# Split weight parts that start at seven places within a 64-byte line

## The chip, the core and the metric

The kernel runs on one core of a Trainium2 chip. The metric is the device time of one execution in microseconds. The core has a matrix engine (TensorE, PE in the profile, with its weight loads listed as PEld), a vector engine (VectorE, DVE), a scalar engine (ScalarE, ACT), a general engine (GpSimd, POOL) and a queue that issues transfers (SyncE, SP). Operands lie in an on-chip memory of 128 partitions (SBUF), results of matmuls in another (PSUM).

## The reference, cut to what matters

Two layers of a decoder trunk over 512 tokens of width 1024, in float32. Each layer is a chain of weight products with attention, a retention branch and gates between them:

```
for l in range(DEPTH):                       # DEPTH = 2
    h  = rmsnorm(x, g_mix)
    z  = h @ w_in                            # 1024 -> 5888 columns, split in nine
    ya = sliding_window_sink_attention(aq, ak, av, sinks) @ w_a
    yb = (rmsnorm_per_head(retention(rq, rk, rv)) * silu(rg)) @ w_b
    x  = x + (sigmoid(ga) * ya + sigmoid(gb) * yb) @ w_out
    h2 = rmsnorm(x, g_mlp)
    x  = x + square(relu(h2 @ w_up)) @ w_down   # 1024 -> 4096 -> 1024
out = rmsnorm(x, g_final)
```

## The kernel before

**Products in two parts.** A float32 product is made from operands cut in two: hi, the value rounded to the matrix engine's single-pass format (float32r), and lo, what is left of it. `products` (L278 to L286) issues three matmuls for each pair of operands: hi times hi (L284), hi times lo (L285) and lo times hi (L286). Each has a stationary operand of 128 by 128, which is loaded first (an LDWEIGHTS in the profile), and a moving operand of up to 512 columns.

**Weight units.** All weights are laid out beforehand in units of 128 partitions by 1,024 floats (`UNIT`), 4,096 bytes in each partition. `order` lists them in the order of use, 158 for each layer, 316 in all. `load_until` (L171) brings a unit's raw values into a tile with the tag `raw`; `split_until` (L216) makes hi from it on ScalarE (L234) and lo on VectorE (L235); `unit` (L240) hands the two parts to the matmuls and keeps the splits up to three units ahead of use. The tags `raw`, `hi` and `lo` belong to the pool `wpool` (L121), which has three buffers of each. A buffer is written again when the matmuls of the unit that held it are done.

**Where they lie.** In the memory layout of the program before, every buffer of `raw`, `hi` and `lo` starts on a multiple of 64 bytes within its partition, and so do the activations' tiles `x`, `xh`, `xl`, the nine tiles `r0` to `r8`, and the temporaries. Allocation is in steps of 32 bytes; a few constants (`sink`, `mask`, `ident`, `half`) start 32 bytes into a 64-byte line. The constant `LINE` (L50) fills the gains in front of `x` up to a multiple of 16 floats. A slice of 128 columns of a unit begins at a multiple of 512 bytes from the unit's start.

**Who uses the parts.** In most products the weight parts are the stationary operand: `chunk` (L318), `group` (L330), `two_chunks` (L346) and the loop over `w_a` (L897) run them against 512 moving columns of activations. `values` (L742) is the reverse: the activations are stationary and the weight parts move, 512 columns at a time, into four banks named `rv`. In the MLP, `pair` (L1027) works out two blocks of `w_up` by a scheme with seven half products in place of eight; its matmuls have 256 moving columns, and a pair's four parts are units whose raw values are sums and differences that `add_part` (L202) makes on VectorE. There are 14 pairs in each layer. In the last layer's end (`end`, L407) the moving columns are also 256; the last five units of the order get their parts in tiles of their own there, `homes` (L224 to L226), and not in `wpool`.

**Order around the change.** Each engine runs its instructions in program order; waits come from the tiles: ScalarE's L234 waits for a unit's transfer and for a free `hi` buffer, VectorE's L235 for L234, the matmuls for both. Retention and attention steps are put between the products by `advance` (L302). Which instruction comes when doesn't depend on where in a buffer a part starts.

Of the kernel before, what the change touches and what calls it, by code (L numbers as in the profile page):

```python
# [11 lines left out]
F32R = mybir.dt.float32r  # L12
# [5 lines left out]
P = 128  # L18
# [26 lines left out]
UNIT = 1024  # L45
WARM = 8
PACE = 0.8
DEEP = 3
DELAY = 2
LINE = -(-(2 * DEPTH + 1) * KD // 16) * 16  # L50


# [63 lines left out]
def decoder(ctx, tc, xT, x_first, w_in, w_a, w_b, w_out, w_up, w_down, sinks, tables, decay, band, out):  # L116
# [4 lines left out]
    wpool = ctx.enter_context(tc.tile_pool(name="wpool", bufs=3))  # L121
# [6 lines left out]
    def f32(ap):  # L128
        return ap.bitcast(F32)
# [12 lines left out]

    n_gain = LINE
    gain_x = const.tile([P, n_gain + KD * T], F32, name="x")
# [12 lines left out]
    def halves(i):  # L157

        return (slice(0, UNIT // 2), slice(UNIT // 2, UNIT)) if i < 3 else (slice(0, UNIT),)
# [11 lines left out]
    def load_until(n):  # L171
        while state["loaded"] < min(n, len(order)):
            i = state["loaded"]
            layer, name, j = order[i][:3]
            if name == "pair":
                load_part(i)
            else:
                raws[i] = raw_tile()
                for at in halves(i):
                    queue = nc.scalar if i == 0 and at.start == 0 else nc.sync  # L180
                    queue.dma_start(raws[i][:, at], weights[name][layer, j][:, at])
                    if i < 3:
                        load_x()
            state["loaded"] += 1
# [17 lines left out]
    def add_part(i):  # L202
        part = order[i][3]
        if part == 0:
            w2 = raws[i + 3]
            nc.vector.tensor_tensor(raws[i][:, RIGHT], w2[:, RIGHT], w2[:, LEFT], ALU.add)
        elif part == 1:
            w1 = raws[i - 1]
            nc.vector.tensor_tensor(raws[i][:, LEFT], w1[:, RIGHT], w1[:, LEFT], ALU.subtract)
        elif part == 2:  # L210
            raws[i] = big("raw3").rearrange("p a t -> p (a t)")
            w1, w2, z2 = raws[i - 2], raws[i + 1], raws[i - 1]
            nc.vector.tensor_tensor(raws[i][:, LEFT], w1[:, LEFT], w2[:, RIGHT], ALU.subtract)
            nc.vector.tensor_tensor(raws[i][:, RIGHT], z2[:, RIGHT], z2[:, LEFT], ALU.subtract)

    def split_until(n):  # L216
        while state["split"] < min(n, len(order)):
            i = state["split"]
            load_until(i + 3)
            paired = order[i][1] == "pair"  # L220
            if paired:
                add_part(i)
            raw = raws[i]
            if homes and i >= len(order) - len(homes):  # L224
                home = homes[len(order) - 1 - i]
                hi, lo = (home[:, 2 * a : 2 * a + 2, :].rearrange("p a t -> p (a t)") for a in range(2))  # L226
            else:
                hi = wpool.tile([P, UNIT], F32R, tag="hi", name="hi")
                lo = wpool.tile([P, UNIT], F32R, tag="lo", name="lo")
            for at in (LEFT,) if paired and order[i][3] == 3 else halves(i):  # L230
                if i == 0 and at.start == 0:
                    nc.vector.tensor_copy(hi[:, at], raw[:, at])
                else:
                    nc.scalar.activation(hi[:, at], raw[:, at], AF.Copy)  # L234
                nc.vector.tensor_tensor(lo[:, at], raw[:, at], f32(hi[:, at]), ALU.subtract)  # L235
            raws.pop(i - 3 if paired else i, None)
            parts[i] = (hi, lo)
            state["split"] += 1

    def unit(name, layer):  # L240
        i = state["next"]
        assert order[i][:2] == (layer, name), (order[i], layer, name)
        state["next"] += 1
        split_until(i + 3)
        return parts.pop(i)
# [238 lines left out]
    def layer_body(layer):  # L484
# [124 lines left out]
        def attention():  # L609
# [18 lines left out]
            def weighted(n):  # L628
                at = slice(n * P, (n + 1) * P)
                both = big("whole")  # L630
                rest, whole = both[:, 0, :], both[:, 1, :]
                for g in range(N_KV):
                    own, other = slice(64 * g, 64 * g + 64), slice(64 - 64 * g, 128 - 64 * g)
                    po = bank(ps_aux, "pv")
                    kbs = (1,) if n == 0 else (0, 1)
                    for kb in kbs:
                        b = n - 1 + kb
                        cols = slice(b * P, (b + 1) * P)
                        p = 2 * g + kb
                        nc.tensor.matmul(po, v_both[g][:, cols], p_h[:, p, :], start=kb == kbs[0], stop=False)  # L640
                        nc.tensor.matmul(po, v_high[g][:, cols], p_l[:, p, :], start=False, stop=kb == 1)  # L641
                    nc.scalar.activation(rest[own, :], po[other, :], AF.Copy)
                    nc.vector.tensor_tensor(whole[own, :], po[own, :], rest[own, :], ALU.add)
                split(a_h[:, :, at], a_l[:, :, at], whole.rearrange("p (c q) -> p c q", q=P))

            for n in range(NB):
# [3 lines left out]
                for c in range(4):  # L650
# [32 lines left out]
                    pend.append((n, c, sm))  # L683
                    if ready and c == 1 + DELAY:
                        weighted(ready.pop())
# [416 lines left out]

    scaled_input(0, 0)
    split_until(1)
    for u in (2, 3):
        for k in (2 * u - 3, 2 * u - 2):
            scaled_input(k, 0)
        split_until(u)
# [83 lines left out]
def _stack(w, of):  # L1192
    return np.ascontiguousarray(np.stack([np.stack(of(m)) for m in w]))
# [24 lines left out]
def _laid_out(x, g_mix, w_in, sinks, w_a, w_b, w_out, g_mlp, w_up, w_down, g_final):  # L1218
# [8 lines left out]
        "xT": xT,  # L1227
        "x_first": np.concatenate([gains, np.zeros((P, LINE - gains.shape[1]), np.float32), xT[:, 0, :]], 1),
        "w_in": _stack(w_in, _w_in_units),
# [28 lines left out]
```

## Time and profile before

| | |
|---|---|
| median of 3 runs | 1516.12 us (1516.02 to 1518.61) |
| the profiled execution, its own time | 1514.21 us |
| its span, first to last instruction | 1512.4 us |
| mean granted TensorE clock | 0.998 |
| weight loads and matmuls | 8,080 each |
| whole units split on VectorE (L235), mean | 280, 1,222 ns |
| whole units rounded on ScalarE (L234), mean | 280, 1,058 ns |
| half units split on VectorE (L235), mean | 34, 689 ns |
| transfers, mean rate | 155.11 MB, 103 GB/s |

A row of the groups gives the line and engine, the operation, what it writes and reads, the shape, the count, the group's busy time in microseconds and the mean of one in nanoseconds, and then the idle time of the engine just before these instructions with what ended it. Matmuls are pipelined: the duration of one covers its way through the array, and several are under way at once, so that their durations add up to more than the span. How fast they follow each other is read from the start times in the timeline, whose columns are the start and the duration in microseconds, the engine, the line, the operation, what it writes and reads, and the shape.

A table by stretch, of the MLP of the first layer, has for each engine the busy time and the number of instructions:

```profile
core 0: us, PE busy (x) PEld busy (x) DVE busy (x) ACT busy (x) POOL busy (x), PEclk, DMA share, GB/s
520.00:755.00 235.00, 235.00 (x1402) 208.57 (x1401) 154.49 (x208) 104.53 (x147) 0.96 (x1) 1.00 0.32 114
```

### The profile page before, as it was taken

The page shows a single profiled execution, that of the slowest core. Times are in us where ns is not written, and L with a number is a line of the kernel's source. Part 1 is how long each engine was busy: PE and PEld are TensorE (multiplying, and loading weights), DVE is VectorE, ACT ScalarE, POOL GpSimd, SP SyncE. Part 2 cuts the span into 40 slices and gives each one's busy share as a digit, 9 for nine tenths or more (in the row PEclk, how much of TensorE's full clock was granted, in tenths as well). Part 3 has the DMA queues.
Part 4 walks back from the last instruction along what each step waited for, and adds up shares of the span by engine and source line. Part 5 has one row for each costly group of instructions (what it writes and reads, how often), then busy time and mean ns, then how long its engine had stood idle before and what let it go on. Part 6 is the DMA issues. An engine that isn't in the chain of part 4 may idle for free.

```text
span 1512.4 us, 20505 instructions
## 1 busy us (share of the span) xinstructions
PE 1500.7 (99%) x8080; PEld 1293.3 (86%) x8080; DVE 1028.3 (68%) x1598; ACT 738.8 (49%) x1163; POOL 2.9 (0%) x13
## 2 busy tenths in 40 slices
PE   9999999999999999999999999999999999999997
PEld 7888888888888999988888888888888899899997
DVE  7877568754697666676678855677448866766674
ACT  6657355632564444444455742555226544444452
POOL 0000000000000000000000000000000000000000
PEclk9999999999999999999999999999999999999999
DMA  6422222133223232223432222222332222223231
GB/s 220 133 84 70 98 84 91 70 125 126 98 71 111 98 112 98 98 98 127 158 127 91 84 84 95 79 85 84 126 125 91 91 96 97 101 100 110 98 112 57
DMA packets 52784, 155.11 MB, mean 103 GB/s; under 512 B 6352, under 2 KB 8528, under 8 KB 52688
## 3 DMA queue, kind: packets, MB, share of 16 engines
q1 hardware_dynamic: 52544, 153.54, 29.3%
q8 instruction: 63, 1.03, 0.3%
q14 instruction: 33, 0.27, 0.1%
q10 hardware_dynamic: 144, 0.26, 0.0%
HBM read 146.96 MB, written 4.19 MB: 100 GB/s over the span
## 4 chain that ended last, share of the span: by engine, by line
PE 98%; ACT 1%; DVE 0%; DMA 0%; issue 0%; DVEq 0%
PE mm L286 29%; PE mm L284 29%; PE mm L285 29%; PE rv L284 2%; PE rv L286 2%; PE rv L285 2%; PE score L655 1%; PE pT L620 1%; PE r L285 1%; PE r L286 1%; PE r L284 1%; PE pv L641 0%; PE pv L640 0%; PE ssq L378 0%; PE ret L285 0%; PE ret L286 0%
## 5 line engine op out<-in xcount | busy, mean ns | idle before, releaser
L234 ACT ACTIVATE hi<-raw 128x1024 fp32r<-128x1024 f32 (+1 forms) x313 | 314.6, 1013 | 512.2 <-PE mm L285 418.7
L235 DVE TENSOR_TENSOR lo<-raw,hi 128x1024 fp32r<-128x1024 f32 (+1 forms) x314 | 362.9, 1164 | 159.7 <-ACT hi L234 158.9
L285 PE MATMUL mm<-r,hi 128*128 128x512 f32 (+1 forms) x1136 | 391.7, 346 | 0.0
L284 PE MATMUL mm<-r,hi 128*128 128x512 f32 (+1 forms) x1136 | 388.5, 345 | 1.3 <-ACT mm L1041 1.3
L286 PE MATMUL mm<-r,lo 128*128 128x512 f32 (+1 forms) x1136 | 388.4, 346 | 0.0
L284 PE MATMUL mm<-xh,hi 128*128 128x512 f32 (+1 forms) x1008 | 356.9, 356 | 0.5 <-ACT xh L294 0.5
L285 PE MATMUL mm<-xl,hi 128*128 128x512 f32 (+1 forms) x1008 | 356.2, 355 | 0.0
L286 PE MATMUL mm<-xh,lo 128*128 128x512 f32 (+1 forms) x1008 | 355.7, 356 | 0.0
L284 PEld LDWEIGHTS mm<-r,hi 128*128 128x128 f32 x1136 | 212.9, 188 | 29.2 <-ACT mm L1041 1.7
L285 PEld LDWEIGHTS mm<-r,hi 128*128 128x128 f32 x1136 | 213.3, 188 | 28.0
L286 PEld LDWEIGHTS mm<-r,lo 128*128 128x128 f32 x1136 | 213.0, 188 | 26.5
L284 PEld LDWEIGHTS mm<-xh,hi 128*128 128x128 f32 x1008 | 189.4, 188 | 27.3 <-ACT xh L294 1.2
L285 PEld LDWEIGHTS mm<-xl,hi 128*128 128x128 f32 x1008 | 189.4, 188 | 26.9
L286 PEld LDWEIGHTS mm<-xh,lo 128*128 128x128 f32 x1008 | 189.3, 188 | 25.6
L1068 DVE TENSOR_TENSOR x<-x,mm 128x512 f32<-128x512 f32 x56 | 37.9, 687 | 35.0 <-PE mm L286 34.9
L286 PE MATMUL rv<-hi,xl 128*128 128x512 f32 x128 | 50.6, 395 | 0.0
L285 PE MATMUL rv<-lo,xh 128*128 128x512 f32 x128 | 50.5, 395 | 0.0
L284 PE MATMUL rv<-hi,xh 128*128 128x512 f32 x128 | 50.5, 396 | 0.0
L284 PE MATMUL mm<-uhi,hi 128*128 128x512 f32 (+1 forms) x128 | 46.6, 366 | 0.0
L285 PE MATMUL mm<-ulo,hi 128*128 128x512 f32 (+1 forms) x128 | 46.4, 364 | 0.0
L286 PE MATMUL mm<-uhi,lo 128*128 128x512 f32 (+1 forms) x128 | 45.8, 365 | 0.0
L1048 DVE SCALAR_TENSOR_TENSOR z<-mm,rstd 128x256 f32<-128x256 f32 x28 | 11.9, 425 | 39.7 <-PE mm L286 39.7
(188 smaller groups left out, 1683.2 us busy)
## 6 DMA issues: line engine op xcount, KB each, us to landing
raw<-w_in_in SPq DMA_DIRECT2D x89, 512.0 KB, 3.2
raw<-w_down_in SPq DMA_DIRECT2D x64, 512.0 KB, 3.2
raw<-w_up_in SPq DMA_DIRECT2D x36, 512.0 KB, 3.2
raw<-w_up_in SPq DMA_DIRECT2D x56, 256.0 KB, 2.7
raw<-w_b_in SPq DMA_DIRECT2D x16, 512.0 KB, 3.2
raw<-w_out_in SPq DMA_DIRECT2D x16, 512.0 KB, 3.4
raw<-w_a_in SPq DMA_DIRECT2D x8, 512.0 KB, 3.3
x<-xT_in SPq DMA_DIRECT2D x15, 256.0 KB, 3.9
```

The costliest lines, as they stand in the source:

```text
L234: nc.scalar.activation(hi[:, at], raw[:, at], AF.Copy)
L235: nc.vector.tensor_tensor(lo[:, at], raw[:, at], f32(hi[:, at]), ALU.subtract)
L284: nc.tensor.matmul(ps, ah, bh, start=start and i == 0, stop=False, **more)
L285: nc.tensor.matmul(ps, ah, bl, start=False, stop=False, **more)
L286: nc.tensor.matmul(ps, al, bh, start=False, stop=stop and i == n - 1, **more)
L620: nc.tensor.transpose(pt[:, i * P : (i + 1) * P], sm[:, at : at + P], ident)
L655: nc.tensor.matmul(ps[:, g * w : (g + 1) * w], q_s[g][:, c, at], part[:, keys], start=i == 0, stop=i == 1)
L1048: nc.vector.scalar_tensor_tensor(z[:, 0, :H], a, 0.0, rms_mlp.value[:, :H], ALU.max, ALU.mult)
L1068: nc.vector.tensor_tensor(x[:, c, :], x[:, c, :], ps, ALU.add)
```

## The change

The hi and lo tiles of `wpool` become 16 floats longer, and the parts are cut out of them at a start that depends on the unit's number: 1, 2, 4, 6, 10, 12 or 14 floats behind the buffer's start, that is 4, 8, 16, 24, 40, 48 or 56 bytes, in turn. Both parts of a unit get the same start. None of the seven is a multiple of 32 bytes; two, 16 and 48, are multiples of 16, and one, 4, is not a multiple of 8. With seven places and three buffers, each buffer meets each place. The raw tiles and the home tiles stay as they were.

```diff
@@ -47,6 +47,7 @@
 PACE = 0.8
 DEEP = 3
 DELAY = 2
+PLACES = (1, 2, 4, 6, 10, 12, 14)
 LINE = -(-(2 * DEPTH + 1) * KD // 16) * 16
 
 
@@ -225,8 +226,10 @@
                 home = homes[len(order) - 1 - i]
                 hi, lo = (home[:, 2 * a : 2 * a + 2, :].rearrange("p a t -> p (a t)") for a in range(2))
             else:
-                hi = wpool.tile([P, UNIT], F32R, tag="hi", name="hi")
-                lo = wpool.tile([P, UNIT], F32R, tag="lo", name="lo")
+                first = PLACES[i % len(PLACES)]
+                hi, lo = (
+                    wpool.tile([P, UNIT + 16], F32R, tag=n, name=n)[:, first : first + UNIT] for n in ("hi", "lo")
+                )
             for at in (LEFT,) if paired and order[i][3] == 3 else halves(i):
                 if i == 0 and at.start == 0:
                     nc.vector.tensor_copy(hi[:, at], raw[:, at])
```

## The prediction

> **What bounds the kernel now.** I read the page's totals and chain first, then the groups of instructions with shapes kept apart, then the timeline in one stretch of each shape. The totals and the chain leave one candidate:
>
> ```profile
> span 1512.4 us, 20505 instructions
> PE 1500.7 (99%) x8080; PEld 1293.3 (86%) x8080; DVE 1028.3 (68%) x1598; ACT 738.8 (49%) x1163; POOL 2.9 (0%) x13
> PEclk9999999999999999999999999999999999999999
> PE 98%; ACT 1%; DVE 0%; DMA 0%; issue 0%; DVEq 0%
> ```
>
> PE is the span. VectorE (DVE), which writes lo, has 484 us of idle time, ScalarE (ACT), which writes hi, 774. The clock is granted in full. So the change counts where it alters the distance between matmul starts. Which matmuls touch hi and lo, and how, is in the groups; the last name behind the arrow is the stationary operand, the one before it the moving one:
>
> ```profile
> L235 DVE TENSOR_TENSOR lo<-raw,hi 128x1024 fp32r<-128x1024 f32 x280 | 340.1, 1222 | 136.9 <-ACT hi L234 136.1
> L234 ACT ACTIVATE hi<-raw 128x1024 fp32r<-128x1024 f32 x280 | 293.8, 1058 | 492.9 <-PE mm L285 399.4 <-issue 70.7 <-PE rv L286 18.3
> L285 PE MATMUL mm<-r,hi 128*128 128x512 f32 x672 | 263.2, 392 | 0.0
> L285 PEld LDWEIGHTS mm<-r,hi 128*128 128x128 f32 x1136 | 213.3, 188 | 28.0
> L284 PE MATMUL mm<-r,hi 128*128 128x256 f32 x464 | 129.6, 280 | 1.3 <-ACT mm L1041 1.3
> L284 PE MATMUL rv<-hi,xh 128*128 128x512 f32 x128 | 50.5, 396 | 0.0
> ```
>
> Adding the rows of this kind: 4,320 matmuls of 512 columns have a split part as stationary operand (six rows of 672, three of 96), 2,496 of 256 columns (three rows of 464, three of 336, three of 32), and 384 of 512 columns have it as moving operand (three rv rows of 128). Their durations (280, 392 ns) overlap their neighbours; what fills the span is the distance between starts, read in the timeline:
>
> ```profile
> 148.17 0.19 PEld L286 LDWEIGHTS rv<-hi,xl 128*128 128x128 f32 x1
> 148.40 0.39 PE L286 MATMUL rv<-hi,xl 128*128 128x512 f32 x1
> 148.40 0.19 PEld L284 LDWEIGHTS rv<-hi,xh 128*128 128x128 f32 x1
> 148.63 0.40 PE L284 MATMUL rv<-hi,xh 128*128 128x512 f32 x1
> ...
> 573.00 0.28 PE L285 MATMUL mm<-xl,hi 128*128 128x256 f32 x1
> 573.00 0.19 PEld L286 LDWEIGHTS mm<-xh,lo 128*128 128x128 f32 x1
> 573.12 0.28 PE L286 MATMUL mm<-xh,lo 128*128 128x256 f32 x1
> 573.12 0.19 PEld L284 LDWEIGHTS mm<-xh,hi 128*128 128x128 f32 x1
> ```
>
> The start times give 229.3 ns on average for a 512-column step, 117.1 for a 256-column one, 233.5 for rv. The next weight load begins as its predecessor's matmul begins, 2 to 3 ns later, and not earlier. How long a load holds its path is seen where the matmuls are shortest:
>
> ```profile
> 196.64 0.19 PEld L285 LDWEIGHTS ret<-r 128*128 128x128 f32 x1
> 196.70 0.28 PE L285 MATMUL ret<-r 128*128 128x128 f32 x1
> 196.75 0.19 PEld L286 LDWEIGHTS ret<-r 128*128 128x128 f32 x1
> 196.82 0.27 PE L286 MATMUL ret<-r 128*128 128x128 f32 x1
> 196.87 0.19 PEld L284 LDWEIGHTS mm<-xh,hi 128*128 128x128 f32 x1
> ```
>
> Loads there follow each other every 110 ns or so (196.64, 196.75, 196.87), for 128 columns. So a 512-column step has some 116 ns to spare behind a load, and a 256-column step nearly none: 3 + 110 is the 113 ns that its quickest fifth shows, and 118 the mean of the rest. This is where a slower weight read would come out undiminished.
>
> **The change part by part.** No instruction is added or removed and no loop, wait or queue is touched: the diff alters the start of hi and lo within their buffers. Six buffers grow by 64 bytes each, so the tiles allocated behind them move by 384 bytes, six lines: the phase within a line stays. The raw tiles, and so every weight DMA, keep their place. Units whose parts go to the five home tiles of the end are untouched. Four uses are left.
>
> *ACT writes hi, DVE reads hi and writes lo.* 4,096 bytes a partition cover 64 lines, or 65 from a place within a line. Spread over DVE's 1,222 ns, a line is 19 ns at most; 280 times that is 5 us, and ACT's is less. It lies in the 484 and 774 idle us, so it costs nothing on the path; uncovered it would be those 5 us. Below nothing has no mechanism. The upper end, each access done twice, is a rival below.
>
> *Weight loads under 512-column matmuls.* 4,320 loads; even doubled to 220 ns they fit into 229. Nothing.
>
> *Weight loads under 256-column matmuls.* 2,496 loads, exposed one for one. The trace has no load from a place inside a line, so the price has bounds. A load reads 512 bytes a partition, eight lines, in 110 ns: 13.7 ns a line, and from inside a line nine are touched, so the upper bound is 13.7 ns. The lower is below nothing: if phases set the beat, all could drop to 113, that is minus 3.8 ns. Between them the nearest row is the two beats of the same step, 113 and 118 ns: what a load that just misses its beat is seen to cost. I take that, 5 ns, as a size only: the same operands go at 118 in the fourth part at 607 us and at 113 at 628 us, so addresses don't set today's beats. 2,496 x 5 = **12.5 us** (bounds -9.5 and +34.2).
>
> *rv, with the split parts moving.* 384 matmuls read 2,048 bytes, 32 lines, in some 224 ns (twice the 229.3 - 117.1 = 112 ns that 256 more columns take): 7 ns a line. The upper bound is 7, the lower minus 3 (the quickest beat); the nearest row again is the neighbouring beats of 512-column steps, 226, 229 and 232, 3 ns apart. 384 x 3 = **1.2 us** (-1.2 to 2.7).
>
> Sum: 12.5 + 1.2 = 13.7 us on the profiled execution's 1514.2 (span 1512.4 and 1.8 around it), 1527.9. The median of the runs is 1.9 above that execution, so the forecast is **1530 us**.
>
> **The rivals.**
>
> *Nothing changes: 1516.* For it: a contiguous run is the same number of elements, and the loads move 4 bytes a column in 0.86 ns, a pace that would not need whole lines. Against it: the 256-column steps have no slack in which to hide even 2 ns (5 us in all).
>
> *A finer line: 1522.* If what is fetched at once is a quarter of 64 bytes, two of the seven places (4 and 12 floats, 16 and 48 bytes) are on a boundary and five pay one piece more in 32: 110/32 = 3.4 ns, x 2,496 x 5/7 = 6.1 us. The Trainium skill's page "SBUF — State Buffer", under "Specifications (TRN2)", gives lines of 16 bytes with a penalty at each cross to a new one, which would be this case; no run here shows the line's length yet.
>
> *A whole line each: 1553.* The upper bounds: 34.2 + 2.7 = 36.9. For it: nothing on PE could hide it. Against it: the ninth line is read only in part.
>
> *The splits become late: about 1576.* If a write or read off the line takes two passes, lo takes 1.07 us longer. Between 520 and 755 us DVE is busy 154.5 of 235 us and holds 64 splits, 55 of them whole; 55 x 1.07 + 9 x 0.53 = 64 us more make 218, too tight beside the pieces that wait for PE. One late split per pair and per block of down, 56 in both layers, x 1.07 = 60 us. It decides once DVE falls a unit behind. Against: DVE's 1,222 ns for 1,024 elements and 688 for 512 is a fixed pace per element.
>
> *Faster: 1504.* One mechanism: the two reads of PE, stationary and moving, start at one phase of a line everywhere, meet, and the slower beats (118, 229 to 232) are what that costs; different phases would keep them apart. All in the quick beat gives 2,496 x 3.8 + 4,320 x 3.3 = 24 us; a reader of seven places would get half, 12 us. It decides if beats follow addresses. Against: the same tiles at both beats above. Also, 512-column steps with DVE and ACT both idle take 229.07 ns (609 of them), with both busy 229.26 (1,403), so engines don't disturb each other's reads. The Trainium skill says the same on the page "SBUF — State Buffer", section "SBUF: two separate sides" (only the port pair of VectorE and GpSimd is contended for), and the trace agrees to 0.2 ns.
>
> **How the numbers follow.** Forecast 0.32; nothing changes 0.26; the finer line 0.10; the whole line 0.10; late splits 0.05; faster 0.15; other costs, either way, 0.02. Slower by over 0.2% (3 us, about what can be told here from no change) sums the four costly cases and half the rest, 0.58; same 0.26; faster 0.16. The likeliest case's own range is 1521 to 1543. The range given starts at 1507, with three quarters of the faster case's way to its middle inside, and ends at 1556, past the whole line; late splits and the better half of the gain stay out.
>
> **What would show it.** 256-column steps of hi or lo longer by some 5 ns, and unlike by place: the unit's number modulo seven should sort them. Steps of 512 columns unchanged, rv by a few ns. The durations of L234 and L235 within 20 ns of 1,058 and 1,222. If the loads' spacing stays 110 and the time rises, the price sits elsewhere. A DVE row near 2,290 ns would be the late splits. Wrong altogether would be 512-column steps that move with hi and lo stationary, since 116 ns of cover would have to vanish; then 4,320 steps count where I have none.

## The result, and the profile after

The changed kernel takes 1530.23 us (median of 4 runs, 1529.2 to 1531.52) against 1516.11 us: 1.009 times as long, with a 95% interval of 1.0072 to 1.0107. The profiled execution took 1529.21 us, its span is 15.0 us longer than before. The totals and the chain of the page after, in the form shown of before:

```profile
span 1527.4 us, 20505 instructions
PE 1515.7 (99%) x8080; PEld 1297.7 (85%) x8080; DVE 1029.0 (67%) x1598; ACT 739.3 (48%) x1163; POOL 2.9 (0%) x13
PE 98%; ACT 1%; DVE 0%; DMA 0%; issue 0%; DVEq 0%
```

The same instructions, PE 15.0 us busier, DVE and ACT busy within 1 us of before. The groups with shapes kept apart, of the changed kernel (three lines further down in the code):

```profile
L238 DVE TENSOR_TENSOR lo<-raw,hi 128x1024 fp32r<-128x1024 f32 x280 | 340.3, 1223 | 139.4 <-ACT hi L237 138.7
L237 ACT ACTIVATE hi<-raw 128x1024 fp32r<-128x1024 f32 x280 | 294.2, 1059 | 504.8 <-PE mm L288 408.8 <-issue 72.7 <-PE rv L289 18.4
L288 PE MATMUL mm<-r,hi 128*128 128x512 f32 x672 | 264.9, 394 | 0.0
L288 PEld LDWEIGHTS mm<-r,hi 128*128 128x128 f32 x1136 | 213.6, 188 | 28.9
L287 PE MATMUL mm<-r,hi 128*128 128x256 f32 x464 | 130.5, 281 | 1.0 <-ACT mm L1044 1.0
L287 PE MATMUL rv<-hi,xh 128*128 128x512 f32 x128 | 50.6, 397 | 0.0
```

The two instructions that write hi and lo take 1 ns longer than before, a weight load is 188 ns as it was, and the matmuls' durations grow by 1 or 2 ns. What grows is the distance between starts. The timeline of PE over 13 units of the same products, from the same matmul to the same matmul, 312 steps; first before, then after (columns: start and duration in us, engine, line, operation, out<-in, shape):

```profile
339.32 0.39 PE L284 MATMUL mm<-xh,hi 128*128 128x512 f32 x1
339.55 0.39 PE L285 MATMUL mm<-xl,hi 128*128 128x512 f32 x1
...
410.73 0.39 PE L284 MATMUL mm<-r,hi 128*128 128x512 f32 x1
```

```profile
342.12 0.40 PE L287 MATMUL mm<-xh,hi 128*128 128x512 f32 x1
342.36 0.39 PE L288 MATMUL mm<-xl,hi 128*128 128x512 f32 x1
...
414.55 0.40 PE L287 MATMUL mm<-r,hi 128*128 128x512 f32 x1
```

71.41 us before and 72.43 after: 228.9 and 232.1 ns a step, in a stretch where the weight load has over 100 ns of cover. Adding up all distances between starts in the two traces, by what the split parts are, gives where the 15 us went (us in all, and ns for one):

```
                                   before           after           difference
4,320 of 512 columns, stationary   995.0  230.3     1006.7  233.0   +11.7
2,496 of 256 columns, stationary   294.6  118.0      297.2  119.1    +2.6
  384 of 512 columns, moving        89.7  233.5       89.8  233.8    +0.1
  879 others                       123.3  140.3      123.8  140.8    +0.5
```

Four fifths lie in the row that the prediction had at nothing. (From here on, wide steps are those of 512 columns, narrow ones those of 256, with a split part as stationary operand.)

### The profile page after: what moved, and what is told of

Same layout as the page of the kernel before. It is cut to its first block, busy times and chain, and to the rows that moved or that the text cites. A ratio compares the mean times of both kernels' runs of the same rounds, so it can differ in the third digit from the quotient of the medians.

```text
span 1527.4 us, 20505 instructions
## 1 busy us (share of the span) xinstructions
PE 1515.7 (99%) x8080; PEld 1297.7 (85%) x8080; DVE 1029.0 (67%) x1598; ACT 739.3 (48%) x1163; POOL 2.9 (0%) x13
## 4 chain that ended last, share of the span: by engine, by line
PE 98%; ACT 1%; DVE 0%; DMA 0%; issue 0%; DVEq 0%
PE mm L287 29%; PE mm L288 29%; PE mm L289 29%; PE rv L287 2%; PE rv L288 2%; PE rv L289 2%; PE score L658 1%; PE pT L623 1%; PE r L288 1%; PE r L289 1%; PE r L287 1%; PE pv L643 0%; PE pv L644 0%; PE ssq L381 0%; PE ret L288 0%; PE ret L289 0%
## 5 line engine op out<-in xcount | busy, mean ns | idle before, releaser
L287 PE MATMUL mm<-r,hi 128*128 128x512 f32 (+1 forms) x1136 | 391.5, 348 | 1.0 <-ACT mm L1044 1.0
L287 PE MATMUL mm<-xh,hi 128*128 128x512 f32 (+1 forms) x1008 | 359.5, 358 | 0.6 <-ACT xh L297 0.6
L287 PEld LDWEIGHTS mm<-r,hi 128*128 128x128 f32 x1136 | 213.2, 188 | 30.8 <-ACT mm L1044 1.4
L287 PEld LDWEIGHTS mm<-xh,hi 128*128 128x128 f32 x1008 | 189.7, 188 | 29.2 <-ACT xh L297 1.1
L287 PE MATMUL rv<-hi,xh 128*128 128x512 f32 x128 | 50.6, 397 | 0.0
L287 PE MATMUL mm<-uhi,hi 128*128 128x512 f32 (+1 forms) x128 | 46.5, 365 | 0.0
```

The lines of the kernel that those rows point to most:

```text
L287: nc.tensor.matmul(ps, ah, bh, start=start and i == 0, stop=False, **more)
```

## The experiments

**Is it the start within a line?** Four kernels with the changed kernel's longer buffers and one place for all units. Their edit is one line, here of the first; the others have 8, 4 and 1:

```diff
-PLACES = (1, 2, 4, 6, 10, 12, 14)
+PLACES = (0,)
```

> The buffers of hi and lo are 16 floats longer, as in the changed kernel, but every part starts at place 0. Theory A, the start within a line is what costs: 1516 us (1514 to 1519), 512-column steps at 229.3 ns on average. Theory B, the layout costs (buffers 65 lines apart in place of 64, everything behind them six lines further on): 1530 us, steps of 512 columns at 232. Theory C, it is the difference of the places from unit to unit: 1516 us.

> Every part starts 8 floats, 32 bytes, behind a line's start. Theory A with a line of 64 bytes: about 1530 us (1526 to 1534). Theory A with pieces of 32 or 16 bytes: 1516 us. Theory C (difference from unit to unit): 1516 us.

> Every part starts 4 floats, 16 bytes, behind a line's start. Theory A with a line of 64 or pieces of 32 bytes: about 1530 us. With pieces of 16 bytes: 1516 us. Theory C: 1516 us.

> Every part starts 1 float, 4 bytes, behind a line's start. Theory A, whatever the size of the pieces: about 1530 us or more, since in the changed kernel units at this place have 512-column steps of 232.7 ns against 229.3 before. Theory C: 1516 us.

```
              us, median   ratio to before, 95% interval
place 0       1529.27      1.0078  1.0061 to 1.0095
place 8       1529.05      1.0080  1.0065 to 1.0095
place 4       1529.64      1.0083  1.0068 to 1.0098
place 1       1535.63      1.0119  1.0104 to 1.0134
```

With every part at place 0, on a line's start, the time is already that of the changed kernel, as theory B had it; A and C had 1516. The start in the line is not what costs, at 16 or 32 bytes; a start of 4 bytes adds 6 us of its own when every unit has it, and one unit in seven has it in the changed kernel. The Trainium skill's page "SBUF — State Buffer" ("Specifications (TRN2)") has lines of 16 bytes, by which place 4 would be as good as place 0 and place 1 dearer; these runs agree on those two, though what a start of 8 bytes costs alone was not tried. The same stretch of 312 steps with place 0 throughout:

```profile
343.87 0.39 PE L287 MATMUL mm<-xh,hi 128*128 128x512 f32 x1
...
416.61 0.39 PE L287 MATMUL mm<-r,hi 128*128 128x512 f32 x1
```

72.74 us, 233.1 ns a step. So the 64 bytes that were added to each buffer carry the loss. They do three things: hi and lo buffers no longer lie a multiple of 4,096 bytes apart, the temporaries move by 384 bytes, and slices no longer start at multiples of 512 bytes.

**Which part of the layout?** One kernel for each of the three, and one that moves lo alone. The first has longer buffers and place 0; the others are the kernel before with unused tiles put in (shown: the third, and the part of the fourth between hi and lo; the second has only a tile of 96 floats in `tmp`):

```diff
-                hi = wpool.tile([P, UNIT], F32R, tag="hi", name="hi")
-                lo = wpool.tile([P, UNIT], F32R, tag="lo", name="lo")
+                hi, lo = (
+                    wpool.tile([P, UNIT + 128], F32R, tag=n, name=n)[:, 0:UNIT] for n in ("hi", "lo")
+                )
```

```diff
+    tmp.tile([P, 112], F32, tag="gap", name="gap", bufs=1)
...
+    const.tile([P, 16], F32, name="front")
```

```diff
                 hi = wpool.tile([P, UNIT], F32R, tag="hi", name="hi")
+                if i == 0:
+                    wpool.tile([P, 16], F32, tag="between", name="between", bufs=1)
```

> The buffers of hi and lo are 128 floats (512 bytes) longer, every part at place 0: all 128-column slices of hi and lo start at a multiple of 512 bytes again, as before, but the six buffers are 4,608 bytes apart and no longer 4,096. Theory D1, what costs is the place of a slice within 512 bytes (or less): 1516 us. Theory D2, the period is longer, up to the 4,096 bytes by which the buffers were apart before: about 1529 us.

> The kernel before, with an unused tile of 384 bytes behind hi and lo, so that only the temporaries move, by as much as in the changed kernel. Theory E, the moved temporaries cost: about 1529 us. Theories D1, D2 and F: 1516 us.

> The kernel before, with 64 bytes in front of raw, hi and lo and 448 behind them: hi and lo keep their distances of 4,096 and 12,288 bytes to each other, all slices start 64 bytes behind a multiple of 512, and the temporaries keep their place within 512. Theory F, a weight load from an address that is no multiple of 512 bytes is slower by itself: about 1529 us or more. Theory G, the distance between the stationary and the moving operand's address decides: not 1516 us, 5 us or more to either side. Theory D, the places of successive weight loads relative to each other decide: 1516 us.

> The kernel before, with 64 bytes between the hi and the lo buffers and 448 behind them: lo's slices start 64 bytes behind a multiple of 512, hi's at one, raw and the temporaries keep their place within 512. Theory D, the places of successive weight loads relative to each other decide (two changes of place in every three loads): about 1529 us. Theory F, each load by itself: a third of the loads, about 1520 us. Theory E: 1516 us.

```
                           us, median   ratio to before, 95% interval
e5 longer by 512 bytes     1515.96      0.9995  0.9986 to 1.0004
e6 temporaries alone       1517.04      1.0002  0.9992 to 1.0011
e7 all parts by 64         1513.27      0.9981  0.9971 to 0.9991
e8 lo alone by 64          1518.02      1.0010  1.0000 to 1.0020
```

The distance of the buffers (D2) and the temporaries (E) fall: both kernels are as before. What is left is the place within 512 bytes. Theory F falls too: in e7 no load starts at a multiple of 512 and the kernel is quicker by 0.2%. That small sum hides two shifts of opposite sign. The stretch of 312 steps in e7, then one of 72 steps of 256 columns (a pair's first six half products), first in the kernel before (L284), then in e7 (L287):

```profile
338.69 0.39 PE L287 MATMUL mm<-xh,hi 128*128 128x512 f32 x1
...
409.41 0.39 PE L287 MATMUL mm<-r,hi 128*128 128x512 f32 x1
```

```profile
572.88 0.28 PE L284 MATMUL mm<-xh,hi 128*128 128x256 f32 x1
...
581.36 0.40 PE L284 MATMUL mm<-r,hi 128*128 128x512 f32 x1
```

```profile
573.60 0.28 PE L287 MATMUL mm<-xh,hi 128*128 128x256 f32 x1
...
582.24 0.40 PE L287 MATMUL mm<-r,hi 128*128 128x512 f32 x1
```

70.72 us or 226.7 ns a wide step, where before it was 228.9; and 8.64 us or 120.0 ns a narrow one, where before it was 8.48 us or 117.8. So one common place 64 bytes further on makes the wide steps quicker and the narrow ones slower. Theory G (the distance to the moving operand) named a change of 5 us or more and got 3, because it did not foresee the two signs. For lo alone by 64, D had 1529 and F 1520; it is 1518, so hi and lo at different places is not by itself the price, or 64 bytes is a cheap difference.

**Hi against lo, and unit against unit.** In the changed kernel, and in the four of the first set, three hi buffers that are 64 bytes longer put lo 192 bytes off hi within 512. The next kernels set that difference alone, and then run through the eight places in one execution, for both parts together and for lo alone:

```diff
+    tmp.tile([P, 80], F32, tag="gap", name="gap", bufs=1)
...
+                if i == 0:
+                    wpool.tile([P, 48], F32, tag="between", name="between", bufs=1)
```

```diff
+                at_hi, at_lo = (16 * ((5 * i + i // 8) % 8),) * 2   # e11: 0, 16 * (...)
+                hi = wpool.tile([P, UNIT + 128], F32R, tag="hi", name="hi")[:, at_hi : at_hi + UNIT]
+                lo = wpool.tile([P, UNIT + 128], F32R, tag="lo", name="lo")[:, at_lo : at_lo + UNIT]
```

> The kernel before, with 192 bytes between the hi and the lo buffers and 320 behind them: every hi slice starts at a multiple of 512 bytes, every lo slice 192 behind one, in all units alike. In the four kernels of 1529 to 1536 us hi and lo of a unit lie 192 bytes apart within 512. Theory D (that difference decides): 1528 to 1532 us, three successive 512-column steps 694 to 700 ns together. Theory H (that units lie differently from each other decides): 1516 us, three steps 687 ns.

> Buffers 512 bytes longer; hi and lo of a unit start at one and the same of eight places (0, 64, ... 448 bytes), which changes from unit to unit. Theory D: 1511 to 1520 us, as the places average, three 512-column steps 684 to 687 ns at 0 and 64. Theory H: 1529 us, with three steps near 694 to 700 ns at every place. The steps by place are also a table of which common place is best.

> As e10, but hi stays at place 0 and lo alone goes through the eight places. Theory D: the unit's place of lo sorts the steps, 687 ns for three at 0, 689 at 64, 694 to 700 at 192, and the time lies between, 1520 to 1528 us. Theory H: about 1529 us and no order by place.

```
                      us, median   ratio to before, 95% interval
e9 lo alone by 192    1526.71      1.0066  1.0051 to 1.0081
e10 both, 8 places    1523.24      1.0045  1.0028 to 1.0062
e11 lo, 8 places      1521.93      1.0030  1.0020 to 1.0040
```

e9 alone has 10 of the changed kernel's 14 us, with the 512-column steps it was to have by theory D (698.6 ns for three) and 256-column steps that got quicker (348.6 against 351.3), which puts it just under D's 1528 to 1532; theory H had 1516. e11 lies in D's range, and its steps at lo's places 0, 64 and 192 are the ones that D named, within 3 ns. e10 is above what theory D allowed, and theory H, by which no place would differ from another, falls on e10's table. Mean time of three successive products of a unit, in ns, by the common place in bytes (e10; the last column is one step with the part moving) and by lo's place with hi at 0 (e11):

```
place        e10: 512 cols   256 cols   rv step      e11: 512 cols   256 cols
  0, 256     689.2  688.5    353  353   233  234     688.2  688.7    351  353
 64, 320     685.1  686.5    359  360   228  229     690.6  691.9    354  354
128, 384     699.3  699.6    350  348   230  230     694.9  692.9    345  347
192, 448     696.8  696.5    357  356   234  233     698.7  697.8    351  350
```

Places 256 bytes apart give the same steps, to within 2 ns in three: the period is 256 bytes, four lines, and each of the four has times of its own. In the program's memory layout nearly all moving operands (`xh`, `xl`, the nine tiles `r`) lie at 64 within 256. That the distance from there matters, and not only the place itself, is seen where the moving operand lies elsewhere, in those blocks of the MLP that move `uhi` and `ulo` out of temporaries: with these at 0 and the weights at 64 (e7), three 512-column steps are 699.9 ns, as with 64 and 128 above (the moving operand's place first, as in the rest of this list); at 0 and 192 (e10) 689.1, as with 64 and 0; at 128 and 0 (e6) 697.2, as with 64 and 192; and 256-column steps at 0 and 0 (before) 359.3, as with 64 and 64. One of these fits badly: 512-column steps at 0 and 0 take 688.7, near 690 in most and 680 in the quickest tenth, where 64 and 64 have 685, and 681 in the same blocks of e12 below. So the distance is the larger part of the order, and not all of it.

Nor does a step go by its own operands alone. In e9 a wide step of hi that is followed by another of hi has its stationary operand, its moving one and the load beneath it at the places that they had before; only lo, in the products around it, lies elsewhere. The median of these steps (1,342 with `xh` or a tile `r` moving) is 229 ns in the trace before, 231 in e8 and 233 in e9. The table above holds for sequences of hi and lo at the places named, and not for single steps.

**A version from the table.** Wide units and rv at distance 0, pairs with hi at 0 and lo at 128:

```diff
+    tmp.tile([P, 16], F32, tag="gap", name="gap", bufs=1)
...
-                hi = wpool.tile([P, UNIT], F32R, tag="hi", name="hi")
-                lo = wpool.tile([P, UNIT], F32R, tag="lo", name="lo")
+                at_hi, at_lo = (0, 32) if paired else (16, 16)
+                hi = wpool.tile([P, UNIT + 64], F32R, tag="hi", name="hi")[:, at_hi : at_hi + UNIT]
+                lo = wpool.tile([P, UNIT + 64], F32R, tag="lo", name="lo")[:, at_lo : at_lo + UNIT]
```

> Places chosen from the tables of e10 and e11. Theory G: the place of the stationary operand within 256 bytes, counted from the moving operand's, sets the step. Nearly all moving operands lie at 64 within 256; the temporaries, some of which move in the last blocks of the MLP, are shifted to 64 too. Units with 512 moving columns, and the values of retention, have hi and lo at 64 (distance 0): three steps 684 ns against 687.5 before, rv steps 227 against 233.5. Units of pairs (256 moving columns) have hi at 0 and lo at 128: three steps 345 ns against 351 before. Sum: 4,320 x 1.2 ns + 384 x 6.3 ns + 2,352 x 2.2 ns = 12.8 us less than before, 1503 us (1498 to 1508). If places don't decide in this way: 1516 us or more.

It takes 1499.12 us (1497.4 to 1499.72), 0.9882 of the kernel before, 0.9865 to 0.9898: quicker than both kernels, and than its own forecast of 1503, inside that forecast's range. Totals, the stretch of 312 wide steps, the 72 narrow ones, and a row of rv:

```profile
span 1497.7 us, 20505 instructions
PE 1485.7 (99%) x8080; PEld 1288.4 (86%) x8080; DVE 1026.7 (69%) x1598; ACT 738.9 (49%) x1163; POOL 2.9 (0%) x13
```

```profile
338.54 0.39 PE L287 MATMUL mm<-xh,hi 128*128 128x512 f32 x1
...
409.26 0.39 PE L287 MATMUL mm<-r,hi 128*128 128x512 f32 x1
...
570.11 0.28 PE L287 MATMUL mm<-xh,hi 128*128 128x256 f32 x1
...
578.27 0.40 PE L287 MATMUL mm<-r,hi 128*128 128x512 f32 x1
```

```profile
L287 PE MATMUL rv<-hi,xh 128*128 128x512 f32 x128 | 49.8, 390 | 0.0
```

226.7 ns a wide step (before 228.9) and 113.3 a narrow one (before 117.8). Summed over the trace, wide steps take 989.3 us, 5.7 less than before, narrow ones 287.3, 7.3 less, rv 87.2, 2.5 less; the others 0.5 more. The forecast had 5.2, 5.2 and 2.4: the narrow steps are what it undervalued, since here nearly every one is on the quick beat (341 to 342 ns for three in the pairs), while the table's 345 and 347 come from units whose neighbours lie at other places; that the neighbours make this difference was not tested by itself. What the shift of the temporaries adds was not separated.

## Why the prediction was right in its time and wrong in its place

- **What bounds the kernel.** Right: PE is the span after too, and the change counts where steps between matmuls alter.
- **ACT and DVE.** Right: 1,059 and 1,223 ns against 1,058 and 1,222; no late splits. (That rival's 56 would by the order of units have been 52, 14 pairs and 12 blocks of `down` in each layer, and 56 us in place of 60.)
- **Weight loads under 512-column matmuls, "Nothing".** This step failed, with the condition named for it ("512-column steps that move with hi and lo stationary"). They have 11.7 of the 15.0 us, 2.7 ns each. The cover of some 116 ns is real, and a load's duration did not grow; but a step is not only a stream plus an uncovered load. Its length changes with the places of hi, lo and the moving operand within 256 bytes, under cover or not: 228.9 ns before, 233.1 in e1 and 226.7 in e7 over the same 312 steps.
- **Weight loads under 256-column matmuls, 12.5 us.** Mis-sized: 1.05 ns each and 2.6 us, of which not all need be the change's, since in e5 and e6, where the parts keep their places within 256 bytes, these steps add up to 1.0 and 1.1 us more than before. "Exposed one for one" found nothing to expose, since a load still takes 188 ns. Nor does the unit's number modulo seven sort the steps by bytes: against the same steps of e1, those of units at 4, 8, 16, 24, 40, 48 and 56 bytes are 0.5, 0.5, 0.6, 1.4, 1.1, 0.5 and 0.8 ns longer.
- **rv, 1.2 us.** 0.1 us. Its units go through quicker and slower places alike.
- **The sum.** 13.7 us forecast on the execution's own time, 15.0 measured, 1530 and 1530.2 in the median. The agreement is chance: two terms were too large by 11 us, and one of 11.7 was missing.
- **The sentence that hid the cause**: that the buffers grow by 64 bytes each and "the phase within a line stays". It was said of the tiles behind; the buffers themselves were moved off each other's place within 256 bytes, and e1 has the whole loss by this, with every part at place 0. What the change says it does, seven places in a line, costs nothing that was seen in the whole (e1 and the changed kernel have spans of 1527.3 and 1527.4 us), though against e1 narrow steps take 1.9 us and rv 1.0 us more in all, and wide ones 2.5 us less; only 4 bytes for every unit cost more.
- **The finer and the whole line.** Both rivals put the price on starts inside a line, and e1 has it without them. That 64 bytes are a unit of what PE reads, by which the bounds of 13.7 and 7 ns were worked out, shows in no run: places 16 and 32 bytes into it cost what place 0 does. The period that the runs show is 256 bytes.
- **The rival for a gain** had the nearer mechanism, the two reads of PE at one phase or at several. Its period was wrong (256 bytes, not 64), and so was the sign for a scatter: before, all lay at the second best of four places for wide steps, and a scatter over places averages 685 to 699 ns for three wide steps. Chosen, not scattered, they give 16.5 us of the 24 that it priced.
- **The evidence against that rival**, one product at 118 ns in one pair and 113 in a later one with the same tiles, was no evidence on addresses: two beats at one place remain in e10 too, at 128 and 384. What chooses between them is open.
- **DVE's and ACT's reads don't matter**: right. In the changed kernel 512-column steps take 232.0 ns with both engines idle and with both busy.

That PE's two streams meet in the memory is argued from this (the steps follow the operands' places, and are as long with DVE and ACT idle as with both busy), and not shown. By e9's steps of hi, neither a step's own weights nor the load that runs beneath it set its length alone; how the products around it act on it is open.

## What to carry to other kernels

Where PE is the bound and steps are a few per cent over their stream, look at how stationary and moving operands lie to each other within 256 bytes, shape by shape: here, with hi and lo at one place, distance 0 was best for 512 columns and worst for 256. A buffer made longer by a single line moves all that lies behind its first copy; to test a start, keep the buffers a multiple of the period apart, or the experiment changes two things. A time that comes out as forecast says nothing of its terms until they are added up from the trace.

## What was not expected of the hardware

- The places of the operands of successive matmuls, within 256 bytes, move a step between 226.7 and some 233 ns at 512 columns and between 113 and 120 at 256, with weight loads at 188 ns throughout.
- The Trainium skill's page "SBUF — State Buffer" ("Who interferes with whom") has PE's two read ports as independent, with no contention but for the pair that VectorE and GpSimd share. The kernels of this study differ by 36.5 us (1499.1 to 1535.6) in nothing but where hi, lo and the temporaries lie, so that PE's time does depend on its operands' places here, and the measurement decides. Whether it is at the two ports that the time goes, no run shows.
- All parts 4 bytes behind a line's start cost 6 us more than at 0, 16 or 32 bytes.
